# The output projection as seven block products over pairs of token blocks

## Chip, core and metric

The kernel runs on one core of one Trainium2 chip. The metric is the device time of one execution in microseconds (us), the median of several runs. The profile is that of one execution of its own; its times count from the span's start.

## The reference

One layer of a hybrid encoder on 1024 tokens of 1024 channels, in float32. The input is normed (`h`) and projected to ten groups of 512 columns and three groups of 1024 gate logits. Three branches follow (pooling, short convolution, stick-breaking attention), each multiplied by a SiLU gate and projected from 512 to 1024 channels. The end of it is what the change touches:

```python
    gates = jax.nn.sigmoid(merge.reshape(b, s, N_BRANCH, D_MODEL))
    merged = jnp.sum(gates * proj, axis=2)
    out = jnp.einsum('bsd,de->bse', merged, w_out)
    return x + rms_norm(out, g_post)
```

`merged` and `w_out` are both 1024 x 1024.

## The kernel before

**Split operands.** Every float32 operand of a matmul is held as a rounded part and a remainder (`split`: ScalarE casts, then GpSimd or VectorE subtracts). A product is three matmuls: rounded by rounded, rounded by remainder, remainder by rounded. TensorE's time is so many matmuls of 128x128 by 128x512.

**Seven in place of eight.** The input projection already takes two column blocks at once as a 2 x 2 block product with seven products (`run_pair`). `h` lies in quarters `b11`, `b21`, `b22` and sums `t1` to `t4` of them (`build_quarters`), as rounded parts and remainders in the pools `big` (eight tiles) and `quarters` (six tiles). The stationary side comes from a generator, `stationary`: for each pair `pair_parts` loads four raw pieces, forms four totals on VectorE and yields seven split weights, in the order in which `product` takes them with `next_w`, two ahead. `wsp` holds three weights. A product is twelve matmuls into one of five PSUM banks; the helper of the pair (`fin0`, `fin1`) adds it to running sums on VectorE.

**Stages, in order of time.** Norm and transposes; attention, with blocks of the input projection as filler; the attention branch's projection, with the sums of `h` built beside it; four pool pairs with the window sums on VectorE; eight convolution pairs; gate pairs for the attention branch, then gate pairs and branch projections for the pool branch, then for the convolution branch. The gated sums of the branches go to DRAM as `proj_d`, transposed: channel block by channel block, 128 channels on the partitions, tokens along the row. The last four channel blocks stay on chip (`gs`, four tiles of the pool `gates`): their two gate pairs come first, then their four branch projections, each half of which is multiplied by its gate and added to the partial sum `pr`, that is loaded with two buffers (`merged`).

**Output projection before.** `take_merged` splits all eight blocks of `merged`, four of them brought back from DRAM, into the tiles that `h` and its sums have left. `out_weight` splits `w_out`, half by half. `out_products` does 24 matmuls for each of eight token blocks and each half of the columns: `merged` is the stationary side, `w_out` the moving one. `square` sums the squares of a half on ScalarE straight from the bank, `scaled` multiplies it by the post-norm gain, and for the last step (lines 852 to 855) GpSimd forms the inverse root, VectorE scales and adds x, SyncE's queue writes out. The last token block's second half is done in two pieces of 256 columns.

**Order.** A scheduler orders the instructions of each engine from the code's order and its own estimate of when operands and buffers are ready. Each engine and SyncE's queue then run in that order: what waits holds up what stands behind it. Nearly all transfers are issued on SyncE's queue.

## Time and profile before

| | us |
|---|---|
| median of 3 runs | 1019.0 (1018.98 to 1019.54) |
| profiled execution | 1020.24 |
| its span | 1018.5 |
| TensorE busy | 989.4 |
| VectorE busy | 632.8 |
| ScalarE busy | 447.0 |
| GpSimd busy | 450.7 |

The span runs from the first instruction to the last; the execution's own time is a little longer. PE is TensorE, DVE VectorE, ACT ScalarE, POOL GpSimd, SP SyncE. A row of the chain gives its start, its length and the work; a row of groups gives source line, engine, operation, output and input tiles, count, then busy time and mean length in ns, then idle time before and what ended it.

### The profile page before, as it was taken

To read this page: it belongs to the slowest core of one execution; us is meant where nothing else is said; L and a number is where in the kernel's file an instruction comes from. 1 tells how busy PE (TensorE), PEld (TensorE's weight loads), DVE (VectorE), ACT (ScalarE), POOL (GpSimd) and SP (SyncE) were. 2 spreads that over 40 slices of the span, in tenths; PEclk is the share of its full clock that TensorE was granted. 3 is DMA by queue.
4 is the path that set the end of the run, shared out by engine and by line. 5 is a ranking of instruction groups with operands and counts; after the bars stand their busy time and mean duration, and the time that the engine had idled before them with its cause. 6 is when DMAs were issued, how large, how long until landed. Compare 5 with 4: busy or idle time off the path is not lost.

```text
span 1018.5 us, 13271 instructions
## 1 busy us (share of the span) xinstructions
PE 989.4 (97%) x4752; PEld 829.1 (81%) x4752; DVE 632.8 (62%) x847; ACT 447.0 (44%) x871; POOL 450.7 (44%) x359
## 2 busy tenths in 40 slices
PE   4999999999998999999999999999999999999997
PEld 3788888888887888887888888888888888888886
DVE  6556776766776977889776776566333443465133
ACT  6556668658664553333322323343322422354111
POOL 3134443643565005545455454445555565656000
PEclk9999999999999999999999999999999999999999
DMA  6201100100100442221222224455433633166033
GB/s 228 62 22 32 32 22 21 42 21 22 32 23 23 168 157 66 84 83 64 82 62 65 81 71 164 149 197 175 135 124 124 217 121 109 63 209 214 1 125 125
DMA packets 43986, 97.09 MB, mean 95 GB/s; under 512 B 5264, under 2 KB 5520, under 8 KB 43920
## 3 DMA queue, kind: packets, MB, share of 16 engines
q1 hardware_dynamic: 43776, 95.71, 29.0%
q8 instruction: 38, 0.62, 0.2%
q10 hardware_dynamic: 144, 0.52, 0.2%
q14 instruction: 28, 0.23, 0.1%
HBM read 73.15 MB, written 23.07 MB: 94 GB/s over the span
## 4 chain that ended last, share of the span: by engine, by line
PE 88%; ACT 4%; DVE 3%; issue 2%; POOL 2%; DMA 1%; SPq 0%; POOLq 0%; DVEq 0%; ACTq 0%
PE q_ps L541 26%; PE g_ps L541 18%; PE g_ps L189 13%; PE pp L493 13%; PE o_ps L795 8%; PE o L420 3%; PE tp L406 2%; DVE sn L388 1%; PE z L384 1%; PE z L381 1%; ACT sn L385 1%; POOL sp L390 1%; DMA xt<-in_x_dram 1%; DVE xt L275 1%; POOL w_lo L74 1%
## 5 line engine op out<-in xcount | busy, mean ns | idle before, releaser
L74 POOL TENSOR_TENSOR w_lo<-s,w_hi 128x512 fp32r<-128x512 f32 x95 | 132.5, 1396 | 178.2 <-ACT w_hi L73 178.2
L390 POOL TENSOR_TENSOR sp<-sp,sn 128x127 f32<-128x127 f32 (+3 forms) x64 | 80.5, 1260 | 131.0 <-DVE sn L388 66.0
L74 POOL TENSOR_TENSOR w_lo<-s_raw,w_hi 128x512 fp32r<-128x512 f32 x70 | 94.3, 1348 | 92.1 <-ACT w_hi L73 92.0
L388 DVE TENSOR_TENSOR_SCAN sn<-sn,zeros 128x128 f32<-128x128 f32 (+3 forms) x64 | 101.2, 1581 | 46.5 <-ACT sn L385 43.0
L73 ACT CAST w_hi<-s 128x512 fp32r<-128x512 f32 x96 | 59.6, 621 | 131.9 <-PE q_ps L541 63.0
L189 PE MATMUL g_ps<-hh,w_hi 128*128 128x512 f32 x240 | 100.5, 419 | 0.1
L73 ACT CAST w_hi<-s_raw 128x512 fp32r<-128x512 f32 x70 | 43.5, 622 | 127.5 <-PE q_ps L541 60.1
L189 PE MATMUL g_ps<-hh,w_lo 128*128 128x512 f32 x240 | 94.8, 395 | 0.0
L189 PE MATMUL g_ps<-hl,w_hi 128*128 128x512 f32 x240 | 94.7, 394 | 0.0
L74 POOL TENSOR_TENSOR w_lo<-w_raw,w_hi 128x512 fp32r<-128x512 f32 x44 | 66.9, 1521 | 52.2 <-ACT w_hi L73 52.2
L541 PE MATMUL q_ps<-hh,w_lo 128*128 128x512 f32 x224 | 87.2, 389 | 0.8 <-POOL w_lo L74 0.8
L541 PE MATMUL q_ps<-hl,w_hi 128*128 128x512 f32 x224 | 87.2, 389 | 0.0
L541 PE MATMUL q_ps<-hh,w_hi 128*128 128x512 f32 x224 | 87.2, 389 | 0.0
L493 PE MATMUL pp<-yhi,w_lo 128*128 128x512 f32 x192 | 74.7, 389 | 0.0
L493 PE MATMUL pp<-yhi,w_hi 128*128 128x512 f32 x192 | 74.7, 389 | 0.0
L493 PE MATMUL pp<-ylo,w_hi 128*128 128x512 f32 x192 | 74.7, 389 | 0.0
L541 PE MATMUL g_ps<-hh,w_hi 128*128 128x512 f32 x160 | 62.3, 389 | 0.0
L541 PE MATMUL g_ps<-hl,w_hi 128*128 128x512 f32 x160 | 62.3, 389 | 0.0
L541 PE MATMUL g_ps<-hh,w_lo 128*128 128x512 f32 x160 | 62.2, 389 | 0.0
L385 ACT ACTIVATE sn<-z 128x384 f32<-128x384 f32 (+2 forms) x96 | 48.0, 500 | 28.8 <-PE z L384 17.2
L234 DVE TENSOR_TENSOR wl<-tp,wh 128x512 fp32r<-128x512 f32 (+2 forms) x96 | 50.2, 543 | 13.8 <-ACT wh L407 13.2
L407 ACT CAST wh<-tp 128x512 fp32r<-128x512 f32 (+2 forms) x96 | 44.9, 495 | 20.6 <-PE tp L406 15.0
(205 smaller groups left out, 2416.4 us busy)
## 6 DMA issues: line engine op xcount, KB each, us to landing
s_raw<-in_w_in_dram SPq DMA_DIRECT2D x96, 256.0 KB, 2.6
pr<-proj SPq DMA_DIRECT2D x48, 256.0 KB, 3.5
proj<-g SPq DMA_DIRECT2D x20, 512.0 KB, 2.9
w_raw<-in_w_in_dram SPq DMA_DIRECT2D x34, 256.0 KB, 2.6
w_raw<-in_w_branch_dram SPq DMA_DIRECT2D x24, 256.0 KB, 2.6
xt<-in_x_dram SPq DMA_DIRECT2D x8, 512.0 KB, 7.8
proj<-proj SPq DMA_DIRECT2D x8, 512.0 KB, 2.8
wo_raw<-in_w_out_dram SPq DMA_DIRECT2D x16, 256.0 KB, 3.2
```

What stands on the lines that cost most here:

```text
L73: nc.scalar.copy(hi, raw)
L74: eng.tensor_tensor(out=lo, in0=raw, in1=f32(hi), op=ALU.subtract)
L189: nc.tensor.matmul(ps, l[:, a], r[k // 4][t][:, k % 4, :], start=(n == 0), stop=(n == 3 * KB - 1))
L234: nc.vector.tensor_tensor(out=o, in0=a, in1=f32(b), op=ALU.subtract)
L385: nc.scalar.activation(sn[:, c0:c1], z[:, :w], AF.Sigmoid, scale=-0.125)
L388: nc.vector.tensor_tensor_scan(out=rev, data0=rev, data1=zeros.to_broadcast([P, n]), initial=1.0, op0=ALU.mult, op1=ALU.max)
L390: nc.gpsimd.tensor_tensor(out=sp[:, 0:n - 1], in0=sp[:, 0:n - 1], in1=sn[:, 1:n], op=ALU.mult)
L407: nc.scalar.copy(wh[c][:, 0:m, qsub], tp[:, 0:m, :])
L420: nc.tensor.matmul(o[:, cs], vc[:, j, s, :], wt[j // 4][:, j % 4, cs], start=(j == 0 and wt is wl), stop=(j == i and wt is wh))
L493: nc.tensor.matmul(pp, l[:, a], r[:, HALVES[t]], start=(n == 0), stop=(n == 3 * NB - 1))
L541: nc.tensor.matmul(bank, l[:, a], r[:, j, :], start=(n == 0), stop=(n == 11))
L795: nc.tensor.matmul(ps, l[:, a], r[:, es], start=(d == 0 and n == 0), stop=(d == KB - 1 and n == 2))
```

## The change

The output projection becomes four calls of `run_pair`, each over two neighbouring token blocks. Its moving side is `w_out` in quarters, `b11`, `b21`, `b22`, and four sums of quarters, `t1` to `t4`; they take the tiles of `h`'s quarters and sums, each as soon as the last gate pair has used the old one. Its stationary side is `merged`, a token block pair at a time, from a third kind of entry in the plan, "tokens" (`token_parts`): the first four channel blocks come from DRAM (`mg_d`) as one 128x512 piece, the last four lie on chip as four tiles, so that totals and splits that touch them are done in four pieces of 128x128.

The sums of `w_out` are formed in float32 by `out_quarters` (16 VectorE differences), written to DRAM (`wq_d`) and read back with the quarters in 28 loads by `out_quarter`, which splits each on ScalarE and alternately on GpSimd and VectorE. `Finish` takes the place of the helpers at the end: sum from PSUM, square, variance, gain, and after the second half inverse root, scaling, adding x and writing out. Pieces of 256 columns are no longer used. The branch projections are the same, but for the destination and how far ahead the weights are taken.

```diff
@@ -118,6 +120,7 @@
     plan += [("branch", KB + d) for d in range(4, KB)]
+    plan += [("tokens", i) for i in range(0, S // P, 2)]
@@ -144,6 +147,44 @@
+    def token_parts(i):
+
+
+        i0, i1 = (slice(n * P, (n + 1) * P) for n in (i, i + 1))
+        a11, a21 = [wraw.tile([P, HALF], F32, tag="raw", name="m_raw") for _ in range(2)]
+        for a, ts in ((a11, i0), (a21, i1)):
+            nc.sync.dma_start(a.rearrange("p (a b) -> p a b", a=4), held["mg"][:, :, ts])
+        a12, a22 = [[m[:, ts] for m in held["m"]] for ts in (i0, i1)]
+
+        def total(a, b, how):
+            o = held["sum"].tile([P, HALF], F32, tag="s", name="s")
+            if isinstance(a, list) or isinstance(b, list):
+                for j in range(4):
+                    nc.vector.tensor_tensor(out=cols(o, j), in0=cols(a, j), in1=cols(b, j), op=how)
+            else:
+                nc.vector.tensor_tensor(out=o, in0=a, in1=b, op=how)
+            return o
...
+        yield weight(a11, nc.gpsimd)
+        s1 = total(a21, a22, ALU.add)
+        s2 = total(s1, a11, ALU.subtract)
+        yield weight(s2, nc.gpsimd)
+        yield weights(a12)
+        yield weight(total(a11, a21, ALU.subtract), nc.gpsimd)
+        yield weight(s1, nc.gpsimd)
+        yield weights(a22)
+        yield weight(total(a12, s2, ALU.subtract), nc.gpsimd)
@@ -693,8 +734,31 @@
+    def out_quarters(j):
...
+        def minus(o, a, b, q):
+            nc.vector.tensor_tensor(out=o, in0=a, in1=b, op=ALU.subtract)
+            nc.sync.dma_start(wq_d[q][:, j, :], o)
+            return o
+
+        q12, q11, q22 = raw(j, HALVES[1]), raw(j, HALVES[0]), raw(4 + j, HALVES[1])
+        d1 = minus(q11, q12, q11, 0)
+        minus(q12, q22, q12, 2)
+        d2 = minus(q22, q22, d1, 1)
+        q21 = raw(4 + j, HALVES[0])
+        minus(q21, q21, d2, 3)
+
     for d in range(0, KB, 2):
         prs = parts_in_dram(d)
+        out_quarters(d // 2)
@@ -713,146 +777,102 @@
-    m_parts = {}
-
-    def take_merged(d, ts, m):
...
-    gated(y_conv, 2)
-    gs = gate_pair() + gate_pair()
...
+    gated(y_conv, [mg_d[:, d, :] for d in range(4)])
+    held["mg"], held["m"] = mg_d, gate_pair() + gate_pair()
+
+
+    def out_quarter(pool, tag, src):
+        hi, lo = [pool.tile([P, 4, HALF], F32R, tag=tag, name=f"o{x}") for x in "hl"]
+        for j in range(4):
+            raw = held["raw"].tile([P, HALF], F32, tag="raw", name="wo_raw")
+            nc.sync.dma_start(raw, src(j))
+            split(raw, hi[:, j, :], lo[:, j, :], (nc.gpsimd, nc.vector)[j % 2])
+            yield hi, lo
...
+    loads = coming()
     for d in range(4, KB):
-        merged(y_conv, d, gs[d - 4], parts_in_dram(d), take)
-    take_merged(*waiting.pop(0))
-    for _ in coming_back:
+        prs = parts_in_dram(d)
+        for _ in range(5):
+            next(loads)
+        merged(y_conv, d, held["m"][d - 4], prs, None, (2, 2, 1, 1)[d - 4])
+    for _ in loads:
         pass
...
+        def __call__(self, t, ps, add):
+            es = HALVES[t]
+            o = self.o[:, es]
+            added(o, ps, add)
+            junk = fin.tile([P, HALF], F32, tag="junk", name="junk")
+            ssq = fin.tile([P, 1], F32, tag="ssq", name="ssq", bufs=4)
+            nc.scalar.activation(junk, o, AF.Square, accum_out=ssq)
...
+            nc.vector.tensor_tensor(out=o, in0=o, in1=gpost_sb[:, es], op=ALU.mult)
...
+    for i in range(0, S // P, 2):
+        run_pair(Finish(i), Finish(i + 1))
```

Line numbers in the changed kernel are higher: `added` is line 588 before and 629 now, a total for a pair's weights 133 and 136, a partial sum's load 687 and 728, its addition 720 and 784. The scheduler moves what the change adds, so three places show the order.

VectorE, third pool pair, from the second pair's `pl` (the remainder of the pooled values) on. `u` and `v` are sums from PSUM, `s` totals for weights, `wo_raw` rows of w_out. Before:

```order
L74 TENSOR_TENSOR pl<-pb_4183,ph 128x1024 [waits Activation_49]
L588 TENSOR_TENSOR u_4370<-g_ps,m_4369 128x512 [waits PE_49]
L661 MEMSET pb_4363 128x16 [waits DVE_49]
L133 TENSOR_TENSOR s<-s,s_raw 128x512 [waits DMAHW6_49,Pool_49]
L588 TENSOR_TENSOR u<-g_ps,m_4369 128x512 [waits PE_49]
L609 TENSOR_TENSOR sig<-u,sig 128x512 [waits DMAHW1_49,Activation_49]
L588 TENSOR_TENSOR u_4371<-q_ps,u_4370 128x512 [waits PE_49]
L133 TENSOR_TENSOR s<-s_raw 128x512 [waits Pool_49]
L588 TENSOR_TENSOR u_4370<-q_ps,u_4370 128x512 [waits DVE_49,PE_49]
L588 TENSOR_TENSOR v<-q_ps,u_4371 128x512
L588 TENSOR_TENSOR v<-q_ps,u_4371 128x512 [waits PE_49]
```

The same place now, from the second of its weights' totals on:

```order
L136 TENSOR_TENSOR s<-s,s_raw 128x512 [waits DMAHW1_49,Pool_49]
L629 TENSOR_TENSOR u<-g_ps,m_4369 128x512 [waits PE_49]
L748 TENSOR_TENSOR wo_raw<-wo_raw 128x512 [waits DMAHW4_49,DMAHW3_49]
L650 TENSOR_TENSOR sig<-u,sig 128x512 [waits DMAHW2_49,Activation_49]
L629 TENSOR_TENSOR u_4371<-q_ps,u_4370 128x512 [waits PE_49]
L136 TENSOR_TENSOR s<-s_raw 128x512 [waits Pool_49]
L748 TENSOR_TENSOR wo_raw<-wo_raw 128x512 [waits DMAHW6_49,DMAHW7_49,DMAHW2_49,DVE_49]
L629 TENSOR_TENSOR u_4370<-q_ps,u_4370 128x512 [waits DVE_49,PE_49]
L629 TENSOR_TENSOR v<-q_ps,u_4371 128x512
L748 TENSOR_TENSOR wo_raw<-wo_raw 128x512 [waits DMAHW3_49,DMAHW1_49,DVE_49]
L748 TENSOR_TENSOR wo_raw<-wo_raw 128x512 [waits DMAHW1_49,DVE_49]
L629 TENSOR_TENSOR v<-q_ps,u_4371 128x512 [waits PE_49]
```

Four differences of `out_quarters`, which the code has in the attention branch's gate pairs, stand between the pair's sums, and three of them wait for transfers.

SyncE's queue, during the last four branch projections. `wq` are the sums of w_out in DRAM, `mg` the merged blocks, `pr` the partial sums. Before, from the last branch weight's load on:

```order
L84 DMA w_raw<-in_w_branch_dram 128x512 [waits DMAHW4_49,DMAHW1_49,Pool_49]
L743 DMA wo_raw<-in_w_out_dram 128x512 [waits Pool_49]
L687 DMA pr<-proj_3530 128x512 [waits DVE_49]
L743 DMA wo_raw<-in_w_out_dram 128x512 [waits DMAHW7_49,DMAHW3_49,Pool_49]
L743 DMA wo_raw<-in_w_out_dram 128x512 [waits DMAHW5_49,DMAHW0_49,Pool_49]
L687 DMA pr<-proj_3530 128x512 [waits DVE_49]
L743 DMA wo_raw<-in_w_out_dram 128x512 [waits DMAHW4_49,DMAHW2_49,Pool_49]
L842 DMA xr<-in_x_dram 128x1024 [waits DVE_49]
L687 DMA pr<-proj_3531 128x512 [waits DMAHW6_49,DVE_49]
```

Now, from seven rows below that branch weight's load on:


```order
L160 DMA m_raw<-mg 128x4x128 [waits Pool_49]
L805 DMA wo_raw<-wq_5992 128x512 [waits DMAHW4_49,DMAHW3_49,DVE_49]
L805 DMA wo_raw<-wq_5992 128x512 [waits DMAHW5_49,Pool_49]
L805 DMA wo_raw<-wq_5992 128x512 [waits DMAHW6_49,DVE_49]
L805 DMA wo_raw<-wq_5992 128x512 [waits DMAHW7_49,Pool_49]
L728 DMA pr<-proj_3530 128x512 [waits DVE_49]
L805 DMA wo_raw<-in_w_out_dram 128x512 [waits DMAHW0_49,Activation_49]
L728 DMA pr<-proj_3530 128x512 [waits DMAHW1_49,DVE_49]
L805 DMA wo_raw<-in_w_out_dram 128x512 [waits DMAHW3_49,DMAHW2_49,Pool_49]
L805 DMA wo_raw<-in_w_out_dram 128x512 [waits DMAHW4_49,DVE_49]
L805 DMA wo_raw<-in_w_out_dram 128x512 [waits DMAHW5_49,Pool_49]
L728 DMA pr<-proj_3531 128x512 [waits DMAHW7_49,DVE_49]
```

The loads of the partial sums for the sixth and seventh channel block (proj_3530, proj_3531) have moved down the queue, behind loads that wait for a split on GpSimd or VectorE to free a buffer.

VectorE, the end of the last branch projection (`pp` its bank, `g` the gated tile, `m` the split merged block). Before:

```order
L718 TENSOR_TENSOR g<-pp,g 128x512 [waits PE_49]
L720 TENSOR_TENSOR g<-pr,g 128x512 [waits DMAHW1_49,DVE_49]
L74 TENSOR_TENSOR m<-g,m 128x512 [waits Activation_49]
L718 TENSOR_TENSOR g<-pp,g 128x512 [waits PE_49]
L720 TENSOR_TENSOR g<-pr,g 128x512 [waits DMAHW4_49,DVE_49]
```

Now, with the start of the first token pair in it:

```order
L782 TENSOR_TENSOR g<-pp,g 128x512 [waits PE_49]
L784 TENSOR_TENSOR g<-pr,g 128x512 [waits DMAHW0_49,DVE_49]
L167 TENSOR_TENSOR s<-m_raw,g 128x128 [waits DVE_49]
L169 TENSOR_TENSOR s<-s,m_raw 128x512 [waits DVE_49,Pool_49]
L169 TENSOR_TENSOR s<-m_raw 128x512 [waits Pool_49]
L782 TENSOR_TENSOR g<-pp,g 128x512 [waits PE_49]
L784 TENSOR_TENSOR g<-pr,g 128x512 [waits DMAHW1_49,DVE_49]
L167 TENSOR_TENSOR s<-g,s 128x128 [waits Pool_49]
```

The last block's first half is multiplied and added to its partial sum, then the last quarter of the first total and the whole second total follow, which is the stationary side of the pair's second product; the second half comes behind them.

More of the change, by code (lines that the diff above doesn't have):

```diff
@@ L98, in stationary @@
                 yield loaded(w_branch[n], nc.gpsimd)
+            elif what == "tokens":
+                yield from token_parts(n)
             else:
@@ L727, in gated @@
[L727 to L728 removed]
+        branch_proj(ys, next_w(ahead), post, ps_p)
+        if dst is not None:
+            nc.sync.dma_start(dst, g)
+    def gated(ys, dsts):
+        for d in range(0, len(dsts), 2):
             prs = parts_in_dram(d)
             for i, g in enumerate(gate_pair()):
[L731 to L739 removed]
@@ L814, in scaled @@
-    def scaled(ps, o, es):
-        nc.vector.tensor_tensor(out=o, in0=ps, in1=gpost_sb[:, es], op=ALU.mult)
-    kept_o, kept_var = [], []
-    def first_half(i, ps):
-        kept_var.append(square(ps, None))
-        o = (held["raw"].tile([P, HALF], F32, tag="raw", name="o0") if i < 5
-             else held["sum"].tile([P, HALF], F32, tag="s", name="o0"))
-        scaled(ps, o, HALVES[0])
-        kept_o.append(o)
-    n_tok = S // P
-    ahead = [held["q"].tile([P, HALF], F32, tag="q", name="o_ps") for _ in range(3)]
```

144 lines of the change are left out of this document (53 added, 91 removed).

## The prediction, made before the changed kernel had run

> **What bounds the kernel now.** I read the page first: its busy times, the strip of 40 slices and the shares of the chain that ended last.
>
> ```profile
> span 1018.5 us, 13271 instructions
> PE 989.4 (97%) x4752; PEld 829.1 (81%) x4752; DVE 632.8 (62%) x847; ACT 447.0 (44%) x871; POOL 450.7 (44%) x359
> PE   4999999999998999999999999999999999999997
> PEclk9999999999999999999999999999999999999999
> PE 88%; ACT 4%; DVE 3%; issue 2%; POOL 2%; DMA 1%; SPq 0%; POOLq 0%; DVEq 0%; ACTq 0%
> ```
>
> PE is busy in nearly every slice from the second to the last but one, at the full clock, and the chain is PE's for 88% of the span. A busy matmul row alone proves little, since matmuls are pipelined, so I looked next at PE's waits over the whole span.
>
> ```profile
> PE xtp L285 <- DVE xt L275: 10.2, 1, 10.2
> PE xtp L285 <- DVE hl L288: 5.0, 2, 2.9
> PE q_ps L541 <- POOL w_lo L74: 0.8, 1, 0.8
> ```
>
> The two large ones lie in the first 35 us. After 370 us PE waits once, for 0.8 us. So what a matmul costs in the rest is its place in PE's queue, and taking matmuls away shortens the span as long as nothing new is late. The chain in order of time says how much, for the part that is changed:
>
> ```profile
> 900.30 2.72 PE q_ps L541 x12
> 903.02 21.76 PE pp L493 x96
> 924.78 85.04 PE o_ps L795 x389
> 1009.83 2.67 issue
> 1012.50 0.38 ACT late L806
> 1015.04 0.40 DVE o L854
> ```
>
> A product of twelve 128x512 matmuls takes 2.72 us, 0.2267 us each. The last four branch projections run from 903.02 to 924.78. The output projection follows without a gap to about 1012.1; some matmul records are missing near the end, hence "issue". From the last square at 1012.50 to VectorE's end at 1015.44 pass 2.9 us, to the span's end 6.0.
>
> **The change part by part: PE.** The lines of the projection's matmuls, by source line:
>
> ```profile
> L795 PE MATMUL o_ps<-wo,m x216: 278/389/389, 968.1 to 1011.9; 128*128 128x512 f32 x84, 128*128 128x256 f32 x24
> L795 PE MATMUL o_ps<-oh,m x192: 389/389/389, 924.6 to 967.9; 128*128 128x512 f32 x192
> ```
>
> The code asks for 8 token blocks x 2 halves x 8 x 3 = 384 matmuls of 512 columns (24 of them cut into 48 of 256; 24 rows of these are missing here). The new stage has 4 pairs x 7 products x 12 = 336 of 512 columns. 48 x 0.2267 = **10.9 us less**. The four pairs would take 76.2 us, and end at 1000.9 if PE never waits.
>
> **The end of the kernel.** Before, the last piece is 256 columns wide. Now it is a whole half with one more VectorE step, because the square reads the sum and not the bank. And the other token block of the pair finishes just ahead on the same in-order queue. The durations:
>
> ```profile
> L588 DVE TENSOR_TENSOR g<-q_ps,u 128x512 f32<-128x512 f32 x21 | 14.3, 685 | 14.6 <-PE q_ps L541 14.6
> L806 ACT ACTIVATE late<-o_ps 128x512 f32<-128x512 f32 x15 | 9.0, 597 | 57.0 <-issue 52.3 <-PE o_ps L795 4.7
> L806 ACT ACTIVATION_READ_ACCUMULATOR late<-o_ps 128x1 f32 x17 | 3.3, 193 | 0.0
> L811 DVE SCALAR_TENSOR_TENSOR var<-ssq,var 128x1 f32<-128x1 f32 x9 | 1.4, 159 | 26.7 <-ACT late L806 26.7
> L852 POOL TENSOR_TENSOR rstd<-var,expo 128x1 f32<-128x1 f32 x8 | 4.4, 548 | 67.8 <-DVE var L811 67.8
> L854 DVE SCALAR_TENSOR_TENSOR o<-o,rstd,xr 128x512 f32<-128x512 f32 x15 | 10.6, 748 | 1.1 <-POOL rstd L852 0.4
> ```
>
> One finish is sum 0.69, square 0.79, variance 0.16, power 0.55, two scaled sums 1.50: 3.7 us (the product with the gain, about 0.69, lies under square and power). The first token block's finish starts when the sixth product ends, 2.7 us before PE's end, and so holds VectorE until 1.0 us after it; the second then takes 3.7: 4.7 us, against 2.9 before (1012.50 to 1015.44). The last transfer is 256 KB in place of 128 KB, about 0.1 more. **Tail: +2.0 us.** Bounds: +0.8 if the two finishes interleave, +3 with hand-overs.
>
> **Sums of w_out among the pooling.** The scheduler puts the sixteen new VectorE differences (line 748) not into the gate stage, where the code has them, but into the four pool pairs, 371 to 455 us by the old clock.
>
> ```profile
> 370.00:450.00 80.00, 80.00 (x354) 66.15 (x353) 59.34 (x88) 28.34 (x47) 37.64 (x26) 1.00 0.26 83
> 450.00:475.00 25.00, 24.18 (x107) 19.59 (x106) 23.66 (x28) 6.84 (x11) 12.63 (x9) 1.00 0.26 84
> L133 DVE TENSOR_TENSOR s<-s_raw x48: 673/692/1764, 347.5 to 878.8; 128x512 f32<-128x512 f32 x48
> ```
>
> The columns after the length are PE, PEld, DVE, ACT and POOL. VectorE idles 80 - 59.3 = 20.7 us in the first stretch and 1.3 us in the second. The nearest row to the new difference is line 133: same shape, two operands in SBUF, 0.69 us in the median and up to 1.76 when GpSimd is in the way. Sixteen cost 11.0 us at the median and 28.2 at the most. So PE could lose nothing, or 28.2 - 20.7 = 7.5 us. What makes a delay count is this chain, from the timelines of three engines:
>
> ```profile
> 465.41 0.16 DVE L673 TENSOR_TENSOR pb<-phd,v 128x16 f32<-128x16 f32 x1
> ```
> ```profile
> 465.60 1.05 ACT L73 CAST ph<-pb 128x1024 fp32r<-128x1024 f32 x1 [5.27 <-DVE pb L673]
> 466.56 0.62 ACT L73 CAST w_hi<-s_raw 128x512 fp32r<-128x512 f32 x1
> ```
> ```profile
> 467.25 1.97 POOL L74 TENSOR_TENSOR w_lo<-s_raw,w_hi 128x512 fp32r<-128x512 f32 x1 [4.14 <-ACT w_hi L73]
> ```
>
> ScalarE stands 5.27 us before the pooled values, and the next weight's cast is queued behind; its remainder is the one that PE waits 0.8 us for. There VectorE has no reserve left: each us of backlog at 465 is a us of PE. Of the sixteen differences one stands behind the third pool pair's `pl`, and four between the second pair's and the third's, where they must fit into that stretch's idle time. I take **+1.5 us**: one difference of about 1 us with nothing to cover it, and half a us carried over. Ends 0 and 7.5.
>
> The Trainium skill, "SBUF — State Buffer", section "Who interferes with whom", says that a VectorE instruction with two SBUF inputs and a GpSimd instruction that reads SBUF exclude one another, the later one waiting in full. By that rule all sixteen may meet a GpSimd operation, which is the 28.2 us case; the median row says that most do not.
>
> **Into the last stage.** Seven quarters of w_out or its sums are read in 28 loads, and split. The splits start as the last gate pair lets go of h, at 886.7, and the last is wanted in the first token pair, after 940. GpSimd gets 14 of these remainders and 8 of stationary pieces, VectorE 14.
>
> ```profile
> L74 POOL TENSOR_TENSOR w_lo<-s,w_hi 128x512 fp32r<-128x512 f32 x95 | 132.5, 1396 | 178.2 <-ACT w_hi L73 178.2
> ```
>
> 22 x 1.40 = 30.7 us in the 38.1 until 924.78. They fit, with PE's next stationary piece never more than an operation or two ahead of its use. What is late is the merged input. The first token pair's second stationary piece needs the sum of all four late blocks, so the last one's first half:
>
> ```profile
> 921.04 0.33 SPq L687 DMA_DIRECT2D pr<-proj  x1
> ```
> ```profile
> 926.61 0.69 DVE L720 TENSOR_TENSOR g<-pr,g 128x512 f32<-128x512 f32 x1 [0.19 <-DMA pr<-proj]
> ```
> ```profile
> DMA to landing us min/median/max: 3.2/3.6/5.5
> ```
> ```profile
> 903.02:924.78 21.76, 21.76 (x98) 18.02 (x97) 14.91 (x19) 9.32 (x17) 12.34 (x9) 1.00 0.69 217
> ```
>
> Before, that half is added at 926.61, since its partial sum was issued at 921.04 into a full DMA (share 0.69) and took 5.5 us to land. It hurt no one: the old projection took it as the last of eight. Now follow a quarter of a sum, the second sum, a cast and a remainder. For the short ones the nearest rows:
>
> ```profile
> L234 DVE TENSOR_TENSOR wl<-tp,wh 128x128 fp32r<-128x128 f32 x16 | 4.4, 273 | 0.1
> L407 ACT CAST wh<-tp 128x128 fp32r<-128x128 f32 x16 | 4.6, 287 | 0.7 <-PE tp L406 0.7
> L390 POOL TENSOR_TENSOR sp<-sp,sn 128x127 f32<-128x127 f32 x8 | 3.7, 456 | 13.4 <-DVE sn L388 10.7 <-ACT wh L407 2.3 <-ACT sn L385 0.4
> ```
>
> 927.30 + 0.27 + 0.69 + 0.62 = 928.9, where PE wants it at 924.78 + 2.72 = 927.5: 1.4 us late. Its remainder, 1.40 us on, is wanted 0.45 us after that: 0.9 more. Between the last branch weight's load and this partial sum stand sixteen loads of quarters and merged blocks, where there were six and two of x; against that VectorE has no `m` to split any more. I take **+3.0 us** for this place. With the half added right behind its product (923.8) it is 0; with two loads of 5.5 in place of 3.6 us one behind the other it is 2.3 + 3.8, and with the blocked VectorE queue about 7.
>
> **Inside the pairs.** Per pair GpSimd has 5 x 1.40 + 8 x 0.46 + 2 x 0.55 = 11.8 us of 19.0. VectorE has seven sums from PSUM (4.8), four products with the gain (2.8), four scaled sums (3.0), two whole totals (1.4), eight quarter totals (2.2) and four variances (0.6): 14.8 us, up to 19 if half of those with two SBUF operands meet GpSimd. Near full, but the totals for the next pair stand early in the queue, some 8 us ahead of their casts. I take **+0.5 us**, ends 0 and 3.
>
> **Sum.** -10.9 + 2.0 + 1.5 + 3.0 + 0.5 = -3.9 us, on a span of 1018.5: 1014.6. The profiled execution took 1020.24, so it would take 1016.3; the runs' median of 1019.0 is 1.2 below it, and with the same difference becomes **1015 us**.
>
> **The rivals.**
>
> Everything new is covered. For it: PE's one wait after 370 us, and the early building of quarters. Against it: 465 us has no reserve. The sum is then -10.9 + 2.0 + 0.5 = -8.4: 1010.6.
>
> The first token pair's wait costs the clock as well. The half-block arrives 5.5 us after a late issue, PE stands about 7 us in place of 3, and then runs slower for a while. The row for that, after the waits at the start:
>
> ```profile
> 30.00:35.00 5.00, 3.51 (x15) 3.15 (x16) 4.43 (x8) 2.12 (x4) 0.00 (x0) 0.67 0.22 56
> ```
>
> The granted clock (third column from the end) is 0.67 there, so 5 x 0.33 = 1.7 us more. 1015 + 4 + 1.7 = 1020.7. The stall of 0.8 us at 468 lost no clock. The Trainium skill, "TensorE: Matmul & The Clock Gate", section "HAM oscillation", warns of PE gaps above about 3.4 us, after which the clock is halved; by that rule a wait of 3.0 us just escapes and one of 7 does not.
>
> It becomes slower, through VectorE among the pool pairs. `wraw` has three buffers and each block of w_out rows takes four, so the fourth load waits until an earlier difference is written out. The fourth difference stands in VectorE's in-order queue until then, with the totals for PE's weights behind it.
>
> ```profile
> proj<-proj SPq DMA_DIRECT2D x8, 512.0 KB, 2.8
> wo_raw<-in_w_out_dram SPq DMA_DIRECT2D x16, 256.0 KB, 3.2
> ```
>
> One round is 0.7 + 2.8 + 3.2 = 6.7 us, four of them 26.8. The queue holds about 3 us of other work between the differences. If no more covers a round, 26.8 - 12 = 14.8 us in place of 1.5: 1028. It decides once PE stands more than 5.4 us there, which eats what is left of the gain. Against it: the scheduler put seven to twenty VectorE rows between the second and the fourth difference of a block, and VectorE idles 20.7 us anyway.
>
> **Chances.** The forecast 0.55, its own range 1012.5 to 1018; everything covered 0.20; late with the clock 0.15; slower through VectorE 0.10. The range of 8 in 10 is 1010.5 to 1021: it holds the forecast, most of the covered case and most of the late one. A measurement of this kernel can tell about 0.2%, 2.0 us, from no change: 1017.0 to 1021.0. Faster: 0.20, and 0.50 of the forecast's 0.55 (the rest lies between 1017 and 1018): 0.70. The same: 0.05 and 0.10 of the late case: 0.15. Slower: 0.05 of the late case and 0.10: 0.15.
>
> **What would show it.** In the changed profile: 336 matmuls in the last stage at 0.2267 us each; a PE wait on a weight remainder of 1 to 3 us around 460 to 475; one or more waits of about 3 us together within 8 us of the first token pair's start, released by GpSimd or ScalarE after the addition of `pr`; under 1 us of waits in the other three pairs; 8 us from the last matmul to the end. Wrong would be a PE wait between 380 and 450, a granted clock below 1.00 at the first pair, or waits in every token pair.

## The result, and the profile after

The changed kernel takes 1041.7 us in the median of four runs (1038.9 to 1043.9), the kernel before 1019.0 (1018.7 to 1019.5). The ratio is 1.022, with a 95% interval of 1.0207 to 1.0234: slower by 22.7 us, where 4 us faster was forecast. The head of its page and the shares of the chain that ended last:

```profile
span 1042.1 us, 13492 instructions
PE 989.6 (95%) x4680; PEld 819.2 (79%) x4680; DVE 694.6 (67%) x930; ACT 463.6 (44%) x925; POOL 502.2 (48%) x409
PE   4999999999998999889999999999999999988995
PEclk9999999999999999899999999999999999999998
PE 73%; issue 7%; POOL 6%; DVE 5%; ACT 5%; DMA 3%; SPq 0%; POOLq 0%; DVEq 0%; ACTq 0%
```

The strip of PE has two soft places, one from 417 to 469 us (two slices of 8, among the pool pairs) and one from 912 to 964 us (two of 8, the last branch projections and the first token pair), and the chain has lost 15 points of PE. The waits of PE, the larger ones, of which none lies before 380 us (those of the start and of the attention, 21.5 us before and 21.8 now, are left out):

```profile
PE q_ps L582 <- POOL w_lo L74: 6.9, 7, 1.3
...
PE q_ps L582 <- ACT w_hi L73: 3.8, 5, 1.7
PE g_ps L582 <- POOL w_lo L74: 3.3, 4, 1.2
PE pp L534 <- DVE g L782: 2.5, 2, 1.6
PE pp L534 <- POOL w_lo L74: 2.1, 1, 2.1
```

Before, PE waited 0.8 us in this part of the span; these five rows make 18.6 us. The time lost is more than that, since the matmul behind a wait starts late by more than the row says: the one at 951.11 has 1.04 us listed and starts 1.43 us after the one ahead of it, where 0.2267 is usual. Where the waits fall is read by putting the same matmul of both traces side by side. In PE's timeline of the kernel before, the start of the first product behind the fourth pooling product, the first of the last four branch projections, the first of the output projection; then of the changed one the same three, ahead of them the first product of the pool pairs, which stood at 379.24 before, and behind them the last matmul:

```profile
473.08 0.39 PE L541 MATMUL q_ps<-hh,w_hi 128*128 128x512 f32 x1
902.86 0.39 PE L493 MATMUL pp<-yhi,w_lo 128*128 128x512 f32 x1
924.62 0.61 PE L795 MATMUL o_ps<-oh,m 128*128 128x512 f32 x2
```
```profile
377.67 0.39 PE L582 MATMUL q_ps<-t2h,w_hi 128*128 128x512 f32 x1
485.75 0.39 PE L582 MATMUL q_ps<-hh,w_hi 128*128 128x512 f32 x1
920.20 0.50 PE L534 MATMUL pp<-yhi,w_lo 128*128 128x512 f32 x1 [2.12 <-POOL w_lo L74]
947.19 0.39 PE L582 MATMUL q_ps<-oh,w_hi 128*128 128x512 f32 x1
...
1030.98 0.39 PE L582 MATMUL g_ps<-oh,w_lo 128*128 128x512 f32 x1
```

| stretch | later than before at its end | lost in it |
|---|---|---|
| up to the pool pairs | 377.67 - 379.24 = -1.6 | -1.6 |
| pool pairs | 485.75 - 473.08 = 12.7 | 14.2 |
| convolution and gates | 920.20 - 902.86 = 17.3 | 4.7 |
| last four branch projections | 947.19 - 924.62 = 22.6 | 5.2 |
| products of the output projection | 1031.4 - 1012.1 = 19.3 | -3.3 |
| from the last matmul to the end | 1042.1 - 1018.5 = 23.6 | 4.3 |

The last matmul ended at 1012.1 before, as the prediction has it, and ends at 1031.4 now. In the last row but one stand the 10.9 us saved and 7.6 us given back. The 4.7 us of convolution and gates hold a stop at 829 us (1.2 us, absent from the run without sums below) and one at 918 (2.1 us), which belongs to the last stage. The 1.6 us at the top are won ahead of any changed work: in both traces PE waits 2.1 us just after 29 us, but from 30 to 35 us the clock is 0.67 before (the row is in the prediction) and 1.00 now, and the same matmuls take 9.24 us in place of 10.80. Part of all this is no wait, but the clock (third column from the end), in three stretches behind a wait:

```profile
424.30:430.30 6.00, 5.98 (x14) 4.35 (x15) 5.44 (x11) 2.09 (x3) 2.51 (x2) 0.51 0.54 171
921.70:925.20 3.50, 3.50 (x10) 2.73 (x9) 0.36 (x2) 1.46 (x4) 2.62 (x2) 0.51 0.87 260
481.40:484.90 3.50, 3.50 (x10) 2.70 (x9) 3.29 (x4) 0.62 (x1) 1.74 (x3) 0.52 0.36 101
```

Matmuls start 0.43 us apart there in place of 0.2267. Added up row by row, that is 2.9, 1.6 and 1.5 us in the order shown, 6.0 in all.

**How a difference reaches PE.** The longest stop among the pool pairs is at 420.55. VectorE's queue behind the first pooling product, before (that product ran from 409.16) and after (from 408.47):

```profile
410.06 1.45 DVE L652 SCALAR_TENSOR_TENSOR sig<-mx,pscale_sb,sig 128x512 f32<-128x512 f32 x2
411.43 1.22 DVE L666 TENSOR_TENSOR pb<-v 128x1024 f32<-128x1024 f32 x1
412.68 1.23 DVE L666 TENSOR_TENSOR pb<-pb 128x1024 f32<-128x1024 f32 x1
413.83 0.68 DVE L588 TENSOR_TENSOR u<-q_ps,u 128x512 f32<-128x512 f32 x1
```
```profile
410.06 1.77 DVE L136 TENSOR_TENSOR s<-s_raw 128x512 f32<-128x512 f32 x1 [0.60 <-POOL w_lo L74]
411.76 1.77 DVE L748 TENSOR_TENSOR wo_raw<-wo_raw 128x512 f32<-128x512 f32 x1
...
417.02 0.69 DVE L748 TENSOR_TENSOR wo_raw<-wo_raw 128x512 f32<-128x512 f32 x1 [1.69 <-DMA wo_raw<-in_w_out_dram]
417.63 1.40 DVE L693 SCALAR_TENSOR_TENSOR sig<-mx,pscale_sb,sig 128x512 f32<-128x512 f32 x2
...
420.08 0.68 DVE L748 TENSOR_TENSOR wo_raw<-wo_raw 128x512 f32<-128x512 f32 x1
420.68 0.68 DVE L629 TENSOR_TENSOR u<-q_ps,u 128x512 f32<-128x512 f32 x1
```

The sum `u` comes 6.9 us later than before, though PE is not later. Three differences stand ahead of it: one of 1.7 us, one with a wait for its load of 2.3, one of 0.6. What hangs on `u`, on ScalarE, GpSimd and PE:

```profile
421.40 0.63 ACT L649 ACTIVATE sig<-u 128x512 f32<-128x512 f32 x1 [8.14 <-DVE u L629]
421.93 0.60 ACT L73 CAST w_hi<-s 128x512 fp32r<-128x512 f32 x1
```
```profile
422.61 1.65 POOL L74 TENSOR_TENSOR w_lo<-s,w_hi 128x512 fp32r<-128x512 f32 x1 [7.93 <-ACT w_hi L73]
```
```profile
422.59 0.50 PE L582 MATMUL q_ps<-t3h,w_hi 128*128 128x512 f32 x1 [1.65 <-ACT w_hi L73]
...
424.32 0.79 PE L582 MATMUL q_ps<-t3h,w_lo 128*128 128x512 f32 x1 [0.99 <-POOL w_lo L74]
```

ScalarE stands 8 us at the sigmoid of `u`, and the cast of PE's next piece, which needs nothing of it, is queued behind. After the two waits PE has the half clock for 6 us. Most of what is tested below is in these rows: an operation's price is not its length, but what is queued behind it on three engines.

### The profile page after: what moved, and what is told of

The parts are those of the page before. It is cut to its first block, busy times and chain, and to the rows that moved or that the text cites. A ratio compares the mean times of both kernels' runs of the same rounds, so it can differ in the third digit from the quotient of the medians.

```text
span 1042.1 us, 13492 instructions
## 1 busy us (share of the span) xinstructions
PE 989.6 (95%) x4680; PEld 819.2 (79%) x4680; DVE 694.6 (67%) x930; ACT 463.6 (44%) x925; POOL 502.2 (48%) x409
## 4 chain that ended last, share of the span: by engine, by line
PE 73%; issue 7%; POOL 6%; DVE 5%; ACT 5%; DMA 3%; SPq 0%; POOLq 0%; DVEq 0%; ACTq 0%
PE q_ps L582 25%; PE g_ps L582 17%; PE g_ps L230 13%; PE pp L534 10%; POOL w_lo L74 3%; PE o L461 3%; PE tp L447 2%; DVE sn L429 1%; PE z L425 1%; DMA wo_raw<-wq 1%; PE z L422 1%; ACT sn L426 1%; DVE ot L869 1%; POOL sp L431 1%; DMA pr<-proj 1%
## 5 line engine op out<-in xcount | busy, mean ns | idle before, releaser
L74 POOL TENSOR_TENSOR w_lo<-s,w_hi 128x512 fp32r<-128x512 f32 x111 | 158.4, 1429 | 225.4 <-ACT w_hi L73 225.4
L73 ACT CAST w_hi<-s 128x512 fp32r<-128x512 f32 x112 | 69.2, 618 | 136.5 <-PE q_ps L582 56.1
L136 DVE TENSOR_TENSOR s<-s_raw 128x512 f32<-128x512 f32 x48 | 43.0, 896 | 22.1 <-POOL w_lo L74 21.6
```

The costliest lines, as they stand in the source:

```text
L73: nc.scalar.copy(hi, raw)
L74: eng.tensor_tensor(out=lo, in0=raw, in1=f32(hi), op=ALU.subtract)
L136: nc.vector.tensor_tensor(out=o, in0=a, in1=b, op=how)
```

## Experiments: what the saving and the sums are worth

Times are medians of four runs; the kernel before took 1018.6 to 1019.7 beside them. The change's own runs are 5 us apart, so a gain of 2 us over it is no more than likely. Code is shortened to the lines that matter. Where an expectation gives PE longer waits in the change than the rows above do (14, 9.4, 4.3 us), it counts the time lost from one matmul's start to the next.

**The saved matmuls alone**, in the kernel before:

```
 for d in ds:
+    if d == 3:
+        continue
```

> The kernel before, with one of the eight row blocks of w_out left out of the output projection's products: 336 of its 384 matmuls of 512 columns, as many as in the change, and nothing else is touched (the result lacks that block). Measures the term of the saving by itself. Theory (each matmul is worth its place in PE's queue): 48 x 0.2267 = 10.9 us less, 1008 us. Rival (the last stage of the kernel before has another limit than PE just under it, so fewer matmuls don't shorten it as much): 1011 or more.

1007.7 against 1018.6 us: 10.9 us less. The first term of the sum holds to a tenth.

**No sums of w_out.**

```
-        out_quarters(d // 2)
-    sum_quarter: wq_d[q][:, j, :]
+    sum_quarter: the quarter of w_out itself
```

> The sixteen differences of w_out, their sixteen loads and sixteen writes are left out; the four factors that were sums are read as plain quarters of w_out, so the output projection multiplies other numbers, with the same instructions. This prices the building of the sums as a whole. In the profile of the change the projections of the branch end 1.6 us earlier than before the change, and the product behind the fourth pooling product starts 12.5 us later: 14.1 us lost among the pool pairs. Theory (the sums cost that): time 1041.7 - 14 = about 1028, PE waits between 380 and 490 us under 1.5 us in all, granted clock 1.00 there, and the last stage as slow as in the change (so still 9 us slower than the kernel before). Rival (the pool pairs are late from something else, the new order of the queues for instance): over 1036, with waits left there.

1026.5 us: the sums cost 15.2. PE's waits from 380 to 490 us are again those of the kernel before (0.8 us, one).

**Their transfers without the differences, and their differences without the writes.**

```
 def minus(o, a, b, q):
-    nc.vector.tensor_tensor(out=o, in0=a, in1=b, op=ALU.subtract)
     nc.sync.dma_start(wq_d[q][:, j, :], o)
```

> The sixteen VectorE differences are left out; the loads of w_out into the three buffers and the writes of the same buffers to the four scratch tensors stay (the factors of the projection are then plain quarters of w_out). Tells VectorE's time from the transfers and the three buffers. Theory (VectorE's in-order queue: each difference stands ahead of a sum that ScalarE's sigmoid waits for, and the next weight's cast is queued behind that sigmoid): about 1028 to 1030, PE waits between 380 and 490 us under 2 us. Rival (the transfers: the fourth load waits for a write, SP's queue holds the weights' loads back): 1036 or more, with PE waits of 5 us or more there.

```
 def minus(o, a, b, q):
     nc.vector.tensor_tensor(out=o, in0=a, in1=b, op=ALU.subtract)
-    nc.sync.dma_start(wq_d[q][:, j, :], o)
```

> The loads and the sixteen differences stay, the sixteen writes to the scratch tensors are left out, so a buffer is free as soon as VectorE has read it; the factors of the projection are plain quarters of w_out. Theory (VectorE's in-order queue): most of the 14 us stays, 1037 to 1042. Rival (the round of write and load through three buffers): 1028 to 1033.

With the transfers alone 1029.1 us, 2.5 more than with nothing, and no new wait of PE among the pool pairs. With the differences alone 1034.9, 8.4 more, between the ranges of theory and rival. Together they cost 15.2, so some 4 us come from having both, a difference that the scatter of the runs leaves uncertain. PE waits 5.4 us from 380 to 490 in the run without writes, 8.3 in the change. The differences' own row in that run, and in the change with what VectorE idled ahead of them:

```profile
L748 DVE TENSOR_TENSOR wo_raw<-wo_raw x16: 666/688/1772, 371.3 to 432.2; 128x512 f32<-128x512 f32 x16
```
```profile
L748 DVE TENSOR_TENSOR wo_raw<-wo_raw x16: 665/686/1817, 369.9 to 456.6; 128x512 f32<-128x512 f32 x16
...
  DMA wo_raw<-in_w_out_dram: 2.6, 2
```

Without writes the buffers come free sooner and the sixteen are done by 432 us, in the first two pool pairs. With them they reach to 457, into the third, where PE then waits four times (3.4 us in all) in place of once (1.2). VectorE waits for their loads only 2.6 us, and 0.6 in the run without writes, so in this place it is mainly their time: VectorE, then ScalarE, then PE. That time is 17.3 us in the change, not 11, since six of the sixteen are long (see the last section). (All four differences in the list ahead of the prediction name a transfer among what they wait for, not three.)

## Experiments: the same sums elsewhere

**Among the first eight gates**, from a pool of four buffers that opens only when the pool and convolution buffers are given back:

```
+    oqp, close_oq = pool_of("oq", 4)
-            o = wraw.tile([P, HALF], F32, tag="raw", name="wo_raw")
+            o = oqp.tile([P, HALF], F32, tag="oq", name="wo_raw")
```

> Same result as the change. The four buffers of w_out for the differences come from a pool of their own, opened where the pooling and convolution buffers are given back, so loads and differences can't start among the pool pairs; the sixteen differences now stand among the first eight merge gates, where VectorE is busy 138 of 200 us (500 to 700) in the profile before. Theory (the sums cost because VectorE has no reserve between the pooled values and the sums there): about 1028 to 1030, PE waits between 380 and 490 us under 1.5, and under 2 us in the gates. Rival (sixteen differences cost PE wherever they stand, since they and the weights' sums share VectorE's queue): waits of 5 us or more in the gates, 1034 to 1041.

1035.0 us, the rival's number: still 8.5 us for the sums. The pool pairs are as before the change, but PE waits 4.0 us between 560 and 720.

**Among the second eight gates**, through the same three buffers:

```
-        out_quarters(d // 2)                    # first eight gates
+    gated(y_parts_of(yp_d), proj_d, out_quarters)   # behind each pair
```

> Same result as the change. The loads, differences and writes are the same, through the same three buffers, but they stand behind the branch products of the second eight merge gates (about 700 to 800 us), where VectorE is busy under half of the time; four differences fall into each pair of gates. Theory (a difference costs PE only where VectorE's queue has no reserve ahead of a sum that ScalarE and the next weight wait for, or where its load was just issued): no more is lost than without the sums, 1026.5 to 1028.5, PE waits between 380 and 890 us under 2 us. Rival (sixteen differences in the queue of the weights' sums cost PE anywhere, as they did among the first eight gates, where 6 us were lost): 1032 to 1036.

1035.4 us, the rival's number again, though VectorE is busy there less than half of the time.

**On GpSimd**, at the old place:

```
-            nc.vector.tensor_tensor(out=o, in0=a, in1=b, op=ALU.subtract)
+            nc.gpsimd.tensor_tensor(out=o, in0=a, in1=b, op=ALU.subtract)
```

> Same result as the change. The sixteen differences go to GpSimd in place of VectorE, among the pool pairs as before, with the same loads, buffers and writes. GpSimd is busy there for half of the time (12 to 13 of 25 us). Theory (what costs PE is the place of the differences in VectorE's in-order queue, ahead of the sums that ScalarE's sigmoids wait for): PE waits between 380 and 490 us fall from 14 to 4 us or less, 1029 to 1033. Rival (any two-operand work there costs the same, since GpSimd's remainders for PE queue behind its differences and VectorE's operations get longer when GpSimd runs): 1038 to 1045.

1047.5 us, 5.8 more than the change, above the rival's range.

**In the attention stage:**

```
+            if n in (17, 25, 33, 41):
+                out_quarters((17, 25, 33, 41).index(n))
```

> Same result as the change. The same loads, differences and writes through the same three buffers, but asked for in the attention stage, a block of four after each of four steps of it, between about 130 and 280 us, where VectorE is busy 28 to 30 of 40 us, DMA at a tenth, and no sum for PE's next weight stands behind them as among the pool pairs. Theory (the sums cost PE where VectorE has no reserve ahead of something PE's weights wait for): no loss beside the run without sums (1026.5), 1026 to 1029. Rival (sixteen two-operand operations cost PE some 6 to 8 us wherever they stand, as they did among the gates): 1032 to 1036.

1056.3 us, worse than theory and rival: 29.8 us for the sums. This is the place where VectorE idles 10 of 40 us and DMA nine tenths. PE's waits before 380 us grow from 22.1 us (without sums) to 37.5, all of the growth for the attention's own tiles. What the engine of the differences waited for, in the second eight gates, on GpSimd, and in the attention (us, times, longest):

```profile
DVE wo_raw L748 <- DMA wo_raw<-in_w_out_dram: 18.3, 7, 5.2
```
```profile
POOL wo_raw L748 <- DMA wo_raw<-in_w_out_dram: 6.0, 4, 2.3
```
```profile
DVE wo_raw L375 <- DMA wo_raw<-in_w_out_dram: 23.5, 9, 4.3
```

The second row is of 380 to 490 us alone. So in these places something else costs. A difference stands at the head of an in-order queue and waits for its own load, and everything behind it waits along. In the attention the loads share the three buffers with w_in's pieces, and can be issued only when GpSimd has read one: SyncE's queue stands before them for GpSimd 99 us, in eleven places. How much of each price is the waiting, and how much the differences' own time, these runs don't separate.

**Sixteen buffers in place of four**, among the first eight gates:

```
-    oqp, close_oq = pool_of("oq", 4)
+    oqp, close_oq = pool_of("oq", 16)
```

with the four loads of a block asked for ahead of its pair of gates and the differences behind it.

> Same result as the change. As in the run with the differences among the first eight gates (1035.0), but with sixteen buffers in place of four, so that no load of w_out waits for a write, and with the differences asked for behind their pair of gates; in VectorE's queue they stand at nearly the same places, four to eight in each of the first two pairs and the rest in the third. There VectorE stood 5.5 us in four waits for loads of w_out, and PE waited 5.9 us more than without the sums. Theory (what costs is a difference at the head of VectorE's queue that waits for its load): no such waits, PE waits of 2 us or less in the gates, 1026.5 to 1029. Rival (VectorE's time itself): PE waits of 4 us or more in the gates, 1032 to 1036.

1034.2 us, like the four buffers. But the run did not take away what it was meant to, since VectorE waits for these loads as before:

```profile
DVE wo_raw L751 <- DMA wo_raw<-in_w_out_dram: 5.0, 3, 3.0
```

Ahead of the longest of these waits the loads are held back by SyncE's queue, not by buffers: at 622 to 624 us three of them stand behind a load of partial sums and a write that wait for VectorE. How much of the 7.6 to 9 us among the gates is VectorE's time, and how much the wait for loads, stays open.

## Experiments: the last stage

**One quarter in place of seven; all loads, one quarter split.**

```
-    quarters = {"b11": ..., "t2": ..., "b21": ..., "t3": ..., "t1": ..., "t4": ..., "b22": ...}
+    quarters = {"b11": w_quarter(0, HALVES[0])}
```

> Six of the seven quarters (24 of the 28 loads of a quarter's piece, with their casts and remainders on ScalarE, GpSimd and VectorE) are left out in the last stage; all seven products of a token pair use the one that is left, so the output projection gives other numbers with the same instructions on TensorE. Everything else, the sums of w_out too, is as in the change. Prices the building of quarters there. Theory (the pieces' casts and remainders stand in ScalarE's, GpSimd's and VectorE's queues ahead of PE's next weights and of the additions that free the partial sums' buffers): the waits of 9.4 us between 895 and 953 us in the profile of the change fall under 2, 1032 to 1035. Rival (the partial sums are late by their two buffers and their loads alone): over 1038.

```
-            split(raw, hi[:, j, :], lo[:, j, :], (nc.gpsimd, nc.vector)[j % 2])
+            if not only:
+                split(raw, hi[:, j, :], lo[:, j, :], (nc.gpsimd, nc.vector)[j % 2])
```

> In the last stage all 28 loads of pieces of quarters stay, but only the four pieces of one quarter are cast and split; the products all use that one, so the output projection gives other numbers with the same instructions on TensorE. Tells the transfers from the work on the engines. Theory (casts and remainders in the in-order queues of ScalarE, GpSimd and VectorE): 1031 to 1034, like the run with one quarter (1031.6). Rival (the transfers: partial sums and branch weights queue behind 28 loads): 1037 or more, PE waits of 5 us or more between 895 and 953.

1031.6 us with one quarter, 10.2 less than the change; PE does not wait once between 890 and 953 us. With all 28 loads, and one quarter split, 1033.9, and PE waits 0.6 us there. So the building costs 10.2 us: the transfers by themselves cost 2.3, no more than the scatter of the runs, and 7.9 go when the casts and remainders go. ScalarE's and GpSimd's rows of the change show how, ahead of PE's wait of 2.1 us at 920.20:

```profile
916.24 0.62 ACT L73 CAST oh<-wo_raw 128x512 fp32r<-128x512 f32 x1 [0.28 <-DMA wo_raw<-in_w_out_dram]
916.76 0.62 ACT L73 CAST w_hi<-w_raw 128x512 fp32r<-128x512 f32 x1
```
```profile
916.94 1.44 POOL L74 TENSOR_TENSOR ol<-wo_raw,oh 128x512 fp32r<-128x512 f32 x1 [0.26 <-ACT oh L73]
918.34 1.81 POOL L74 TENSOR_TENSOR w_lo<-w_raw,w_hi 128x512 fp32r<-128x512 f32 x1
```

The cast of the first branch weight stands behind casts of quarters that wait for their loads, and its remainder behind one more remainder of a quarter.

**Partial sums aside.** Every second projection's go into two tiles of their own:

```
-        prs = parts_in_dram(d)
+        prs = parts_aside(d) if d % 2 else parts_in_dram(d)   # tiles m1, u2
```

> Same result as the change. Among the last four branch projections the partial sums of every second one are loaded into two tiles of their own (those of the product's intermediate sums, free at that time), so that four halves can be under way in place of two. In the profile of the change three of their loads are issued at 943 to 947 us, after the addition that frees the buffer, PE waits 2.5 us there for VectorE and 2.0 us in the first token pair. Theory (the partial sums are late because their two buffers come free late): these waits fall by 3 us or more, 1036 to 1039. Rival (VectorE and ScalarE are late there with the 28 splits of quarters, and the loads follow them): under 1.5 us gained, 1040 to 1042.

1039.7 us, 2.1 less, between the two. PE's wait before the branch weight falls (2.1 to 0.4), those for the additions do not (2.5 to 3.2).

**More remainders on VectorE:**

```
-(nc.gpsimd, nc.vector)[j % 2]
+(nc.gpsimd, nc.vector)[j > 0]
```

> Same result as the change. Of the quarters' remainders in the last stage three of four are VectorE's, in place of two of four (21 on VectorE, 7 on GpSimd). In the profile of the change GpSimd is busy 20.5 of the 25 us from 900 to 925 and VectorE 12.9, from 925 to 945 it is 13.3 and 16.7 of 20. Theory (GpSimd is the engine that is late, PE's wait of 2.3 us before the first of the last branch products is for its remainder): that wait falls by 1 us or more, 1038 to 1040.5. Rival (VectorE is late from 925 on, and gets seven more operations): PE waits longer for the additions, 1042 to 1046.

1043.7 us, in the rival's range, but no clear difference from the change. PE's first wait is 1.8 in place of 2.1, those for the additions are 4.5 in place of 2.5: what GpSimd was spared was paid on VectorE.

**Variance on ScalarE:**

```
-    o = self.o[:, es]; added(o, ps, add)
+    y = held["raw"].tile(...); added(y, ps, add)
-    nc.vector.tensor_scalar / scalar_tensor_tensor(out=var, in0=ssq, ...)
+    nc.scalar.activation(var, ssq, AF.Identity, scale=1.0 / D, bias=...)
-    nc.vector.tensor_tensor(out=o, in0=o, in1=gpost_sb[:, es], op=ALU.mult)
+    nc.vector.tensor_tensor(out=o, in0=y, in1=gpost_sb[:, es], op=ALU.mult)
```

> Same result as the change. In the finish of a token block the variance is worked out on ScalarE, right behind the square, and the product with the gain goes into another tile than the sum, so VectorE waits for no square; the order of VectorE's queue in a token pair is otherwise the same. In the profile of the change VectorE stands 0.85 us for each of 15 squares, and PE waits 4.3 us in the second to fourth token pair, with 10.9 us from the last matmul's end to the end of the span. Theory (VectorE is the engine that is late in the token pairs, by these waits): PE waits there under 1.5 us, a tail of 8 to 9 us, 1035 to 1037. Rival (GpSimd is late there, with the remainders behind the power): PE waits stay at 3 to 4.5 us, only the tail gets shorter, 1038.5 to 1040.5.

1037.7 us, 4.0 less, just above the theory's range. What VectorE and PE wait for from 953 to 1034 us, in the change:

```profile
DVE var L861 <- ACT junk L858: 6.1, 8, 0.9
DVE var L863 <- ACT junk L858: 5.9, 7, 0.9
DVE ot L869 <- POOL rstd L867: 3.1, 7, 0.4
```
```profile
PE q_ps L582 <- POOL w_lo L74: 1.9, 2, 1.2
PE g_ps L582 <- POOL w_lo L74: 1.2, 1, 1.2
```

and VectorE's largest in this run:

```profile
DVE ot L869 <- POOL rstd L867: 10.2, 8, 1.7
```

The 12 us of waits for squares are gone. Most come back as waits for the power, which stands on GpSimd behind remainders. PE's own fall from 3.4 (the two rows and one of 0.3) to 1.9 us, and the tail from 10.7 to 8.3. The theory's price held for the tail, half for the pairs.

## Experiments: the parts together

> Left out: the sums of w_out with their loads and writes, and six of the seven quarters (as in two earlier runs); and the variance is on ScalarE. So the products of the last stage and the new finish remain, with nearly nothing built for them. Theory (the three places account for the loss and add up): 1041.7 - 15.2 - 8 - 4 = 1014.5, between 1012.5 and 1017, faster than the kernel before, as the saved matmuls say. Rival (part of the saved matmuls' time is lost to something else, as waits in each token pair that come from GpSimd): 1018 or more.

The edits are those of three runs above (no sums, one quarter, variance on ScalarE). 1013.6 us, as expected, against 1018.6 before: the gains over the change, 15.2, 10.2 and 4.0, make 29.4, and 28.1 was measured. With nearly nothing built for them, the seven products gain 5.0 us. So building all sums and quarters would have to cost less than that.

> Same result as the change, with all three edits of this call together (differences among the second eight gates, variance on ScalarE, partial sums of every second projection in tiles of their own). If the three gains add up by the theories: 15 + 5.5 + 4 less than 1041.7, 1016 to 1018.5, level with or just under the kernel before (1019). If only the first holds: 1024 to 1026.

> Same result as the change. Four edits together: the sums among the attention, the variance on ScalarE, partial sums of every second projection in tiles of their own, three of four remainders of the quarters on VectorE. If each does what its theory says and they add up: 1041.7 - 14 - 4 - 2 - 2 = 1020, between 1017 and 1023, level with the kernel before at best, since building quarters keeps most of its 10 us. If the sums cost anywhere: 1025 to 1029.

> Same result as the change, with the sixteen buffers among the first eight gates, the variance on ScalarE and the partial sums of every second projection in tiles of their own. If the loads were what cost: 1027.5 - 4 - 2 = 1021.5, between 1019 and 1024, still not faster than the kernel before, as building quarters keeps its 8 to 10 us. If VectorE's time costs: 1027 to 1031.

Each joins edits shown above. 1030.8 us (sums among the second eight gates; single gains of 6.3, 4.0 and 2.1, which make 12.4, and 11.0 was measured), 1046.1 (sums in the attention) and 1031.7 (sixteen buffers). The first was expected at 1016 to 1018.5, the others at 1017 to 1024, from sums that cost nothing where they were put; the second and third ran over their other forecasts as well (1025 to 1029, 1027 to 1031). No version with the right result beats the kernel before; the best is 1.1% slower, ratio 1.0106, interval 1.0083 to 1.0129.

## Why the prediction was wrong, step by step

**PE, -10.9:** right, 10.9 measured by itself.

**Tail, +2.0 (bounds 0.8 to 3):** mis-sized, 4.3. The step let the first token block's finish start 2.7 us before PE's end. VectorE was behind by then, with a sum, a wait of 0.85 us for a square and a product still ahead, and both finishes ran one behind the other from about PE's end on. Three of VectorE's rows show it, the first block's last sum (PE's last matmul starts at 1030.98), the second's, and its two scalings:

```profile
1031.00 0.68 DVE L629 TENSOR_TENSOR ot<-q_ps,u 128x512 f32<-128x512 f32 x1
...
1035.06 0.68 DVE L629 TENSOR_TENSOR ot<-g_ps,u 128x512 f32<-128x512 f32 x1
...
1037.79 1.41 DVE L869 SCALAR_TENSOR_TENSOR ot<-ot,rstd,xr 128x512 f32<-128x512 f32 x2 [0.44 <-POOL rstd L867]
```

The last sum is taken at 1035.06, 3.7 us after the last matmul. A finish takes 4.1 us in place of 3.7, since the power takes 0.93 us and not 0.55. The step also counted the old tail from the last square, 0.4 us after PE's end, and the new one from PE's end.

**Sums among the pooling, +1.5 (bounds 0 to 7.5):** this is the step that failed most, 15.2. It set the differences' time against VectorE's idle time in the whole stretch, 20.7 us, and even its upper end was half of the truth. Most of that idle time was no reserve, as VectorE's largest waits from 370 to 450 us in the kernel before show:

```profile
DVE s L133 <- POOL w_lo L74: 8.8, 8, 2.8
DVE v L588 <- PE q_ps L541: 2.2, 2, 1.4
```

It stands there ahead of a weight's total until GpSimd has done a remainder, or ahead of a sum until its product is done. Behind the first pooling product, from 410.06 to 421.6 us, it has no gap at all. And the sixteen took 17.3 us, not the 11.0 of the median. The step did name the chain from VectorE through ScalarE's queue to the remainder that PE waits for, and that there is no reserve; but it charged one difference of sixteen to it, while PE's stops at 400, 421, 447 and 478 us show such a place in each pair. (The last of these stood in the kernel before with 0.8 us.) The clock was left out too, 4.4 us of the loss here.

The rival "slower through VectorE" had the size, 14.8 us, and 0.10 of the chances. Its mechanism, the round of write and load through three buffers, is less than half of it: without any write 8.4 us remain, and VectorE waits only 2.6 us for loads there. So the size was in good part luck. Its objection to itself, that VectorE idles 20.7 us anyway, was the same error.

**Into the last stage, +3.0 (0 to 7):** 10.2 us for building quarters. The step counted GpSimd's time (30.7 of 38.1 us) and found that it fits. It priced one place, the last partial sum, and there it was right. VectorE's row of that addition, and PE's of the pair's second product:

```profile
948.51 0.69 DVE L784 TENSOR_TENSOR g<-pr,g 128x512 f32<-128x512 f32 x1 [1.25 <-DMA pr<-proj]
```
```profile
951.11 0.50 PE L582 MATMUL q_ps<-oh,w_hi 128*128 128x512 f32 x1 [1.04 <-ACT w_hi L73]
```

With 0.6 us more at 952.46 the first token pair loses 2.2 us, of 3.0 forecast. What the step had at nothing are the stops before it, 2.1 us at the first branch weight and 2.5 at the additions that hand back PSUM, and 1.6 us of half clock. With one quarter split and all loads in place they are gone but for 0.6 us, so they come mainly from casts and remainders in three in-order queues, which the step had counted as fitting.

**Inside the pairs, +0.5 (0 to 3):** PE waits 3.4 us in pairs two to four, and 7.6 us of the saving are given back in the stage as a whole. The sum of VectorE's work, 14.8 of 19 us, was near (59.2 us busy of the 78 from 953 on). What it lacked are VectorE's own waits: 0.8 us for each square and 0.4 for each power, 13.9 us up to PE's end, and 4.6 for GpSimd ahead of the totals. With them VectorE's queue has no time left.

**What would show it wrong** named three signs: a PE wait between 380 and 450, a clock below full near the first pair, waits in every token pair. The first came. The clock was full in the first pair; the half clock came just ahead of it, in the first of the four branch projections. Waits came in the first, third and fourth pair, none in the second (968.5 to 987.6 us), so the third sign came in part.

The Trainium skill, "TensorE: Matmul & The Clock Gate", section "HAM oscillation", puts the limit of a harmless gap at about 3.4 us. The trace differs: clock 0.51 for 3.5 us after a wait of 2.1 us at 920.20, and for 6 us after waits of 1.65 and 0.99 us close together. The measurement decides here.

## What to carry to other kernels

Idle time of an in-order engine, added up over a stage, is no reserve: look for the one stretch where a product's sum, a sigmoid and the next weight's cast follow one another, and price every new operation by what is queued behind it there. An operation that waits for its own load at the head of a queue holds up everything behind it (up to 5.2 us here ahead of 0.69 us of work), and moving it to an emptier stage doesn't help as long as its load is late there too. Where PE's saving is 1% and the preparation is some seventy operations on three engines, first run the products with the preparation left out: here that gave 5.0 us, the most the change could gain.

## What was not expected of the hardware

PE's clock fell to half after stops of only about 2 us. It happened in the change at three places (6.0 us), and in the runs above too. Not every such stop did it: one of 1.6 us, for an addition at 937 us, left the clock full. The same stop can even go both ways: two waits of 0.9 and 1.2 us in the third pool pair left it full in the change (1.00 from 455 to 458 us) and brought it to 0.50 in the run with one quarter (456.5 to 459.5), and the wait of 2.1 us at the start did so in the kernel before and not in the change. What decides it is open, and so a part of any difference of 1 to 2 us above can be chance.

A difference of two operands in SBUF took about 0.69 us in ten of the sixteen cases and 1.6 to 1.8 in six; these six all had a remainder of GpSimd under way. On GpSimd itself it took 1.3 us, and the kernel was 5.8 us slower: moving work between these two engines gained nothing in the two runs that tried it (this one, and the one with more remainders on VectorE).
